# A diffusion backbone on one core: products and row sums of the adaLN chunks tied to TensorE's progress

## The chip, the cores and the metric

The kernel runs on one core of one Trainium2 chip. The metric is the device time of one execution in microseconds (us). A core has TensorE (PE, matmuls into PSUM), VectorE (DVE), ScalarE (ACT), GpSimd (POOL) and SyncE (SP), which here issues all transfers between HBM and SBUF. Each engine works through its own instructions in order, and semaphores tie the engines together.

## The reference

Two layers over 512 latent tokens of width 1024: layer 0 mixes with windowed attention (256 context tokens beside it), layer 1 with a short gated convolution. Each layer is

```
sh1, sc1, g1, sh2, sc2, g2 = split(silu(c) @ ada_w[i] + ada_b[i])      # six chunks of 1024
h = h + g1 * mixer(rms_norm(h) * gain * (1 + sc1) + sh1)
a = rms_norm(h) * gain * (1 + sc2) + sh2
g, u = split(dwconv3(a @ w_up))                                         # 2 x 2816 wide
h = h + g2 * ((silu(g) * u) @ w_down)
```

All is in float32. The six chunks of a layer (the adaLN modulation) are the product of one vector, silu(c), with a 1024 x 6144 matrix. This text is about seven of these chunks, the last of layer 0 (g2) and all six of layer 1.

## The kernel before

Activations are kept transposed, with features on the 128 partitions and the 512 tokens along the free dimension; h is 8 tiles of 128x512. Each float32 operand of a large matmul is split into a high and a low part (`split`, L163: ScalarE casts to `hi`, VectorE subtracts to get `lo`), and one block product is three matmuls (`mm3`, L195 to L198). A weight tile of 128x1024 is loaded by SP into `wraw` (4 buffers, L172) and split into `whi` and `wlo` (4 + 3 buffers during the FFNs, `wpiece`, L177).

Up to L670 the start and the window attention run in an order written out by hand. Behind that, from the output projection to the end, the order on each engine is made by the framework's scheduler, which follows the program's order as a priority and places an instruction earlier where its engine is free and its inputs are ready by its own reckoning. An instruction with a dependency on another can't be placed ahead of it, and waits for it on a semaphore.

The stretch around the change, in order:

- The output projection of the attention (`out_proj` called at L799). Its first four tiles come from weights at hand; then `last_cols` (L787) closes a chunk of layer 0. It ends by spreading silu(c) over all partitions as a row, `crow` (128x1024): eight TensorE transposes into two PSUM banks and two ScalarE copies (L792 to L796). The last four tiles run in two halves of 256 tokens, and in the second half the norm of the first half begins (`norm_half`, L741; `rstd`, L209, with a root on ScalarE; `modulate`, L230, with VectorE at L233 and L235 and ScalarE at L234). The sums of squares of the first tiles are added on POOL (L207), those of the others on VectorE.
- The first FFN (`ffn`, L801). The 22 pairs of hidden tiles (j and j + 22) are done in thirds of 8, 8 and 6 pairs. A pair is two up projections of 24 matmuls (the first two pairs together, in halves, with the norm's second half hooked in), a convolution over tokens of each (`conv`, L724: ScalarE L725, VectorE L726 and L727), a silu (L818), a product (L819) and a split (L821). After each third the down projection (`out_proj` at L828) runs over its hidden tiles into 8 output tiles, each added into h on VectorE (L736). PSUM has 8 banks, taken in turn (`nbank`).
- The chunks beside it. `adaq` (L677) lists 7 x 8 tiles, each 128 columns of a chunk. For a tile, `ada_tile` (L679) loads 512 KB of transposed weights into one of three buffers `araw` and multiplies them by `crow` on POOL (L684); `ada_sum` (L691) sums the rows on ScalarE, with an activation that has an accumulator (L694), and behind a chunk's eighth tile VectorE adds the bias (L696). `tail0` (L833) is called with 2 after each pair but the first and with 1 after each down tile of the first two thirds. For each tile it first writes out the sums of all products but the last one, then the next product. Only the very first product has a dependency, on the last `modulate` of the norm so far.
- `after_ffn0` (L841) writes out the sums that are left and makes layer 1's scales; the rest of layer 1 (gated convolution, second FFN) uses the same loops without chunk work.

Of the kernel before, what the change touches and what calls it, by code (L numbers as in the profile page):

```python
# [9 lines left out]
DEP = mybir.DependencyInfo(mybir.DependencyClass.Sync, mybir.DependencyReason.DATA)  # L10
AF = mybir.ActivationFunctionType
# [3 lines left out]
P = 128  # L15
# [3 lines left out]
KT = D // P  # L19
# [75 lines left out]
def kernel(ctx: ExitStack, tc: tile.TileContext, xT, ctxT, par_d, rope_d, mask_d, ident_d,  # L95
                         ada0_d, ada_d, adat_d, wqkv_d, wo_d, wup_d, wdown_d, wsc_d, wsco_d, out_d):
    nc = tc.nc
    vec, act, pool, pe, sp = nc.vector, nc.scalar, nc.gpsimd, nc.tensor, nc.sync
# [8 lines left out]
    def nm(s):  # L107
        uid[0] += 1
        return f"{s}{uid[0]}"
# [4 lines left out]
    def bank(tag):  # L114
        if tag == "s":
            return spool[0].tile([P, 512], F32, tag="s", name=nm("ps_s"), bufs=4)
        return pp.tile([P, 512], F32, tag=tag, name=nm("ps_" + tag), bufs=BANKS[tag])
# [7 lines left out]
    def nbank():  # L125
        t = ring[ringpos[0] % 8]
        ringpos[0] += 1
        return bank(t)
# [12 lines left out]
    ident = cp.tile([P, P], F32, name="ident")  # L141
# [7 lines left out]
    cs = cp.tile([P, KT, 2], F32, name="cs")  # L149

    def pc(name, i, n=1):
        o = PC[name][0] + i
        return par[:, o:o + n]
# [41 lines left out]
    def mm3(ps, wh, wl, ah, al, start, stop):  # L195
        pe.matmul(out=ps, lhsT=wh, rhs=ah, start=start, stop=False)  # L196
        pe.matmul(out=ps, lhsT=wh, rhs=al, start=False, stop=False)  # L197
        pe.matmul(out=ps, lhsT=wl, rhs=ah, start=False, stop=stop)  # L198

    def sumsq_add(acc, x, first, eng):  # L200
        if first:
# [41 lines left out]
    def ada_transpose(acc, ps):  # L243
        for i in range(4):
            pe.transpose(out=ps[:, i * P:(i + 1) * P], in_=acc[:, i * P:(i + 1) * P], identity=ident)
        return ps

    def ada_columns(ch, half, ps):
        col = ada[0][:, ch, half * 4:half * 4 + 4]
        vec.tensor_reduce(out=col, in_=ps.rearrange("p (a b) -> p a b", a=4), axis=AX.X, op=ALU.add)  # L250
        vec.tensor_tensor(out=col, in0=col, in1=pc("adab", ch * KT + half * 4, 4), op=ALU.add)

    def scale_cols(dst, sc, gain):
        vec.scalar_tensor_tensor(out=dst, in0=sc, scalar=1.0, in1=gain, op0=ALU.add, op1=ALU.mult)
# [417 lines left out]
    with tc.tile_pool(name="ffn", bufs=1, reuse_waits="tile") as fp, four_banks() as sp3:  # L672
# [3 lines left out]

        adaq = [(0, 5, m) for m in range(KT)] + [(1, ch, m) for ch in (1, 0, 4, 3, 2, 5) for m in range(KT)]  # L677

        def ada_tile(after=None):  # L679

            layer, ch, m = adaq.pop(0)
            w = fp.tile([P, 1024], F32, tag="araw", name=nm("araw"), bufs=3)
            sp.dma_start(out=w, in_=adat_d[6 * layer + ch - 5, m])
            ins = pool.tensor_tensor(out=w, in0=w, in1=crow, op=ALU.mult)  # L684
            if after is not None:
                tc.add_manual_dep(ins.ins, after.ins.name, DEP, reason="the norm has VectorE's port for itself")
            adaps.append((layer, ch, m, w))

        adaps = []

        def ada_sum():  # L691
            layer, ch, m, w = adaps.pop(0)
            col = ada[layer][:, ch, :]
            act.activation(out=w, in_=w, func=AF.Copy, accum_out=col[:, m:m + 1])  # L694
            if m == KT - 1:
                vec.tensor_tensor(out=col, in0=col, in1=pc("adab", (layer * 6 + ch) * KT, KT), op=ALU.add)  # L696

# [9 lines left out]
        def proj(pieces, ah, al, halves=False, group=None, hook=None):  # L707

            n = len(pieces)
            nk = len(ah)  # L710
            group = n if group is None else group
            banks = [nbank() for _ in pieces]
            for hf in (HALVES if halves else (FULL,)):
                for m0 in range(0, n, group):
                    for kt in range(nk):
                        if hook is not None and kt == HOOK_AT and hf.start == 0:
                            hook()
                        ks = slice(kt * P, (kt + 1) * P)
                        for m in range(m0, m0 + group):
                            wh, wl = pieces[m]  # L720
                            mm3(banks[m][:, hf], wh[:, ks], wl[:, ks], ah[kt][:, hf], al[kt][:, hf], kt == 0, kt == nk - 1)
            return banks
# [15 lines left out]
        def norm_begin(slot, shift):  # L738
            return {"acc": f(), "slot": slot, "shift": shift, "ah": [at() for _ in range(KT)], "al": [at() for _ in range(KT)]}
# [6 lines left out]
        def out_proj(src, n, ah, al, gate, nxt=None, last=False, lead=(), tail_w=None, after=None, cols=None):  # L746
# [26 lines left out]
            for hf in HALVES:  # L773
                for i, m in enumerate(ms):
                    if nxt is not None and hf.start and i == HALF_AT:
                        norm_half(nxt, HALVES[0])
                    for kt in range(nk):
                        ks = slice(kt * P, (kt + 1) * P)
                        mm3(banks[i][:, hf], pieces[i][0][:, ks], pieces[i][1][:, ks], ah[kt][:, hf], al[kt][:, hf], kt == 0, kt == nk - 1)
                    residual(m, banks[i], gate, hf)  # L780
                    done(m, hf)
# [3 lines left out]
        crow = fp.tile([P, 1024], F32, name="crow")  # L785

        def last_cols():  # L787
            banks = [ada_transpose(accs[2, hf], nbank()) for hf in range(2)]
            for hf in range(2):
                ada_columns(4, hf, banks[hf])  # L790
            scale_cols(smod[:, 2, :], ada[0][:, 4, :], pc("gffn", 0, 8))
            for half in range(2):  # L792
                ps = nbank()
                for i in range(4):
                    pe.transpose(out=ps[:, i * P:(i + 1) * P], in_=cs[:, half * 4 + i, 0:1].broadcast_to([P, P]), identity=ident)
                act.copy(out=crow[:, half * 512:(half + 1) * 512], in_=ps)  # L796

        nf = norm_begin(2, ada[0][:, 3, :])
        out_proj(lambda m: wo_d[m], 1024, o_hi, o_lo, ada[0][:, 2, :], nf, False, lead, lead_tail, cols=last_cols)  # L799

        def ffn(layer, ah, al, tail, nxt, second):  # L801
# [26 lines left out]
                out_proj(lambda m: wdown_d[layer, m, :, j0 * P:j1 * P], (j1 - j0) * P, hh, hl, gate, nx, fin, after=None if fin else tail)  # L828
            return nx

        held = [True]

        def tail0(n):  # L833
            for _ in range(n):
                while len(adaps) > 1 or adaps and not adaq:
                    ada_sum()
                if adaq:
                    ada_tile(nf["end"] if held else None)
                    held.clear()

        def after_ffn0():  # L841
            assert not adaq
            while adaps:
                ada_sum()
            scale_cols(smod[:, 3, :], ada[1][:, 1, :], pc("gmix", 8, 8))
            scale_cols(smod[:, 4, :], ada[1][:, 4, :], pc("gffn", 8, 8))
            return norm_begin(3, ada[1][:, 0, :])

        n1 = ffn(0, nf["ah"], nf["al"], tail0, after_ffn0, lambda: norm_half(nf, HALVES[1]))
        ah, al = n1["ah"], n1["al"]  # L850

# [91 lines left out]
```

## Time and profile before

| | |
|---|---|
| time, median of 3 runs | 1251.68 us (1250.4 to 1255.4) |
| profiled execution, its own time | 1252.96 us |
| its span, first to last instruction | 1251.2 us |
| mean granted TensorE clock | 0.984 |
| busy: PE, DVE, ACT, POOL | 1196.5, 744.7, 540.3, 302.1 us |
| products of the chunks (L684, POOL) | 56, 150.0 us |
| row sums of the chunks (L694, ACT) | 56, 59.2 us |

The profile is one execution taken by the hardware profiler. A busy time counts an engine's instructions, with waits for a port inside an instruction included; idle time is put down to the instruction that released the engine. In rows of the timeline the columns are start, duration, engine, line, operation, output <- inputs, and in brackets the idle time ahead of it and its releaser. In rows of groups they are line, engine, operation, names, shapes and count, then busy time and mean duration in ns, then the idle time ahead and what ended it. Rows of waits have the total, the count and the longest. PEld is the loading of weights, which overlaps the matmuls. Some matmul records are missing from a trace, so counts of matmuls in a window are good to a few per cent.

### The profile page before, as it was taken

To read this page: it belongs to the slowest core of one execution; us is meant where nothing else is said; L and a number is where in the kernel's file an instruction comes from. 1 tells how busy PE (TensorE), PEld (TensorE's weight loads), DVE (VectorE), ACT (ScalarE), POOL (GpSimd) and SP (SyncE) were. 2 spreads that over 40 slices of the span, in tenths; PEclk is the share of its full clock that TensorE was granted. 3 is DMA by queue.
4 is the path that set the end of the run, shared out by engine and by line. 5 is a ranking of instruction groups with operands and counts; after the bars stand their busy time and mean duration, and the time that the engine had idled before them with its cause. 6 is when DMAs were issued, how large, how long until landed. Compare 5 with 4: busy or idle time off the path is not lost.

```text
span 1251.2 us, 16317 instructions
## 1 busy us (share of the span) xinstructions
PE 1196.5 (96%) x6366; PEld 978.2 (78%) x6366; DVE 744.7 (60%) x1107; ACT 540.3 (43%) x899; POOL 302.1 (24%) x204
## 2 busy tenths in 40 slices
PE   8999999996997499999999999999999999999998
PEld 6676666696886288888888988889988888888888
DVE  4688788658677745663455754444686446553552
ACT  4434777536656554432334442232454224422430
POOL 0069598425638893000001000001000000000000
PEclk9999999998999599999999999999999999999999
DMA  9445143345467674332323233322243333332211
GB/s 361 158 153 171 60 152 118 97 161 171 145 235 229 227 265 144 111 101 86 92 76 105 81 118 101 93 92 69 67 143 93 101 95 91 102 101 85 79 39 68
DMA packets 50317, 157.60 MB, mean 126 GB/s; under 512 B 5696, under 2 KB 7744, under 8 KB 50240
## 3 DMA queue, kind: packets, MB, share of 16 engines
q1 hardware_dynamic: 50240, 156.56, 38.9%
q8 instruction: 50, 0.82, 0.3%
q14 instruction: 27, 0.22, 0.1%
HBM read 152.86 MB, written 2.10 MB: 124 GB/s over the span
## 4 chain that ended last, share of the span: by engine, by line
PE 78%; DVE 7%; issue 4%; POOL 4%; ACT 3%; DMA 3%; SPq 0%; POOLq 0%; DVEq 0%; ACTq 0%
PE ps_s L197 11%; PE ps_s L198 11%; PE ps_s L196 11%; PE ps_pt L196 5%; PE ps_pt L198 5%; PE ps_pt L197 5%; PE ps_oa L629 3%; PE ps_pt L610 3%; PE ps_oa L196 3%; PE ps_oa L197 3%; PE ps_oa L198 3%; PE ps_qt L198 3%; PE ps_qt L197 3%; PE ps_qt L196 3%; DMA araw<-in_adat 3%
## 5 line engine op out<-in xcount | busy, mean ns | idle before, releaser
L165 DVE TENSOR_TENSOR wlo<-wraw,whi 128x1024 fp32r<-128x1024 f32 (+2 forms) x194 | 226.4, 1175 | 186.9 <-ACT whi L164 182.4
L164 ACT CAST whi<-wraw 128x1024 fp32r<-128x1024 f32 (+2 forms) x194 | 183.1, 952 | 284.5 <-PE ps_s L197 124.2
L197 PE MATMUL ps_s<-a,whi 128*128 128x512 f32 (+1 forms) x480 | 176.7, 368 | 0.0
L198 PE MATMUL ps_s<-a,wlo 128*128 128x512 f32 (+1 forms) x480 | 176.5, 368 | 0.0
L196 PE MATMUL ps_s<-a,whi 128*128 128x512 f32 (+1 forms) x480 | 176.5, 368 | 0.0
L684 POOL TENSOR_TENSOR araw<-araw,crow 128x1024 f32<-128x1024 f32 x56 | 150.0, 2700 | 62.6 <-DMA araw<-in_adat 59.7
L196 PE MATMUL ps_s<-g,whi 128*128 128x512 f32 (+1 forms) x296 | 107.1, 362 | 22.2 <-ACT g L164 22.2
L197 PE MATMUL ps_s<-g,whi 128*128 128x512 f32 (+1 forms) x296 | 106.6, 361 | 3.7 <-DVE g L165 3.7
L198 PE MATMUL ps_s<-g,wlo 128*128 128x512 f32 (+1 forms) x296 | 106.1, 359 | 0.0
L198 PEld LDWEIGHTS ps_s<-a,wlo 128*128 128x128 f32 x480 | 90.5, 188 | 15.1
L197 PEld LDWEIGHTS ps_s<-a,whi 128*128 128x128 f32 x480 | 90.5, 188 | 14.9
L196 PEld LDWEIGHTS ps_s<-a,whi 128*128 128x128 f32 x480 | 90.4, 188 | 14.9
L197 PE MATMUL ps_pt<-a,whi 128*128 128x512 f32 (+1 forms) x256 | 94.8, 370 | 2.5 <-DVE a L235 2.5
L207 POOL TENSOR_TENSOR f<-f,t 128x512 f32<-128x512 f32 x6 | 9.5, 1580 | 359.1 <-ACT t L206 359.1
L196 PE MATMUL ps_pt<-a,whi 128*128 128x512 f32 (+1 forms) x256 | 94.7, 370 | 0.7 <-ACT a L234 0.7
L198 PE MATMUL ps_pt<-a,wlo 128*128 128x512 f32 (+1 forms) x256 | 94.5, 369 | 0.0
L694 ACT ACTIVATE araw<-araw 128x1024 f32<-128x1024 f32 x56 | 59.2, 1057 | 60.7 <-POOL araw L684 60.4
L196 PEld LDWEIGHTS ps_s<-g,whi 128*128 128x128 f32 x296 | 57.5, 194 | 32.0 <-ACT g L164 23.4
L736 DVE SCALAR_TENSOR_TENSOR h<-ps_s,ada,h 128x512 f32<-128x512 f32 (+1 forms) x44 | 28.5, 651 | 88.7 <-PE ps_s L198 88.7
L164 ACT CAST g<-f 128x512 fp32r<-128x512 f32 x52 | 32.2, 620 | 99.5 <-DVE f L819 98.9
L197 PEld LDWEIGHTS ps_s<-g,whi 128*128 128x128 f32 x296 | 57.4, 194 | 13.6 <-DVE g L165 4.9
L198 PEld LDWEIGHTS ps_s<-g,wlo 128*128 128x128 f32 x296 | 57.4, 194 | 8.3
(301 smaller groups left out, 2592.8 us busy)
## 6 DMA issues: line engine op xcount, KB each, us to landing
wraw<-in_wup SPq DMA_DIRECT2D x88, 512.0 KB, 3.6
araw<-in_adat SPq DMA_DIRECT2D x56, 512.0 KB, 4.0
wraw<-in_wdown SPq DMA_DIRECT2D x32, 512.0 KB, 3.6
araw<-in_ada SPq DMA_DIRECT2D x48, 256.0 KB, 2.7
wraw<-in_wsc SPq DMA_DIRECT2D x24, 512.0 KB, 3.6
gw<-in_ada SPq DMA_DIRECT2D x16, 512.0 KB, 10.2
wraw<-in_wqkv SPq DMA_DIRECT2D x12, 512.0 KB, 7.0
wraw<-in_wdown SPq DMA_DIRECT2D x16, 384.0 KB, 3.1
```

Source lines behind the costliest of these rows:

```text
L164: act.copy(out=hi, in_=raw)
L165: vec.tensor_tensor(out=lo, in0=raw, in1=hi.bitcast(F32), op=ALU.subtract)
L196: pe.matmul(out=ps, lhsT=wh, rhs=ah, start=start, stop=False)
L197: pe.matmul(out=ps, lhsT=wh, rhs=al, start=False, stop=False)
L198: pe.matmul(out=ps, lhsT=wl, rhs=ah, start=False, stop=stop)
L207: eng.tensor_tensor(out=acc, in0=acc, in1=sq[:, :n], op=ALU.add)
L610: pe.transpose(out=pt[:, q:q + P], in_=es[p, b, t][0][:, o:o + P], identity=ident)
L629: pe.matmul(out=r["po"][HALF[t], b0:b0 + n], lhsT=V[:, j, p // 2, :], rhs=pf[:, t * n:(t + 1) * n], start=first, stop=not r["left"])
L684: ins = pool.tensor_tensor(out=w, in0=w, in1=crow, op=ALU.mult)
L694: act.activation(out=w, in_=w, func=AF.Copy, accum_out=col[:, m:m + 1])
L736: vec.scalar_tensor_tensor(out=h[m][:, cl], in0=ps[:, cl], scalar=gate[:, m:m + 1], in1=h[m][:, cl], op0=ALU.mult, op1=ALU.add)
```

## The change

Each product and each row sum gets a dependency on a matmul. `mm3` keeps its last matmul in `lastmm`; `tail0` passes the one written last, which is the last of the up tile or down tile behind which it is called. At each call the sums of all products so far come first and then the new products, so that a sum is one call behind its product. The spread of silu(c) leaves `last_cols` and is written out at the first call of `tail0`, behind the first two pairs. The old dependency of the first product on the norm goes.

```diff
-        pe.matmul(out=ps, lhsT=wl, rhs=ah, start=False, stop=stop)
+        lastmm[0] = pe.matmul(out=ps, lhsT=wl, rhs=ah, start=False, stop=stop)
...
-        def ada_tile(after=None):
+        def ada_tile(after):
...
             ins = pool.tensor_tensor(out=w, in0=w, in1=crow, op=ALU.mult)
-            if after is not None:
-                tc.add_manual_dep(ins.ins, after.ins.name, DEP, reason="the norm has VectorE's port for itself")
+            pace(ins, after)
             adaps.append((layer, ch, m, w))
...
+        def pace(ins, after):
+            tc.add_manual_dep(ins.ins, after.ins.name, DEP, reason="not ahead of TensorE")
+
-        def ada_sum():
+        def ada_sum(after):
...
-            act.activation(out=w, in_=w, func=AF.Copy, accum_out=col[:, m:m + 1])
+            pace(act.activation(out=w, in_=w, func=AF.Copy, accum_out=col[:, m:m + 1]), after)
...
             scale_cols(smod[:, 2, :], ada[0][:, 4, :], pc("gffn", 0, 8))
-            for half in range(2):
-                ps = nbank()
-                for i in range(4):
-                    pe.transpose(...)
-                act.copy(out=crow[:, half * 512:(half + 1) * 512], in_=ps)
...
-        held = [True]
+        def spread_c():
+
+            for half in range(2):
+                ps = nbank()
+                for i in range(4):
+                    pe.transpose(out=ps[:, i * P:(i + 1) * P], in_=cs[:, half * 4 + i, 0:1].broadcast_to([P, P]), identity=ident)
+                act.copy(out=crow[:, half * 512:(half + 1) * 512], in_=ps)
 
         def tail0(n):
+
+            if len(adaq) == 7 * KT:
+                spread_c()
+            while adaps:
+                ada_sum(lastmm[0])
             for _ in range(n):
-                while len(adaps) > 1 or adaps and not adaq:
-                    ada_sum()
                 if adaq:
-                    ada_tile(nf["end"] if held else None)
-                    held.clear()
+                    ada_tile(lastmm[0])
 
         def after_ffn0():
             assert not adaq
             while adaps:
-                ada_sum()
+                ada_sum(lastmm[0])
```

The code of `spread_c` is that which stood in `last_cols`.

More of the change, by code (lines that the diff above doesn't have):

```diff
@@ L197, in mm3 @@
         pe.matmul(out=ps, lhsT=wh, rhs=al, start=False, stop=False)
-        pe.matmul(out=ps, lhsT=wl, rhs=ah, start=False, stop=stop)
+        lastmm[0] = pe.matmul(out=ps, lhsT=wl, rhs=ah, start=False, stop=stop)
+    lastmm = [None]
     def sumsq_add(acc, x, first, eng):
@@ L791, in last_cols @@
             scale_cols(smod[:, 2, :], ada[0][:, 4, :], pc("gffn", 0, 8))
-            for half in range(2):
-                ps = nbank()
-                for i in range(4):
-                    pe.transpose(out=ps[:, i * P:(i + 1) * P], in_=cs[:, half * 4 + i, 0:1].broadcast_to([P, P]), identity=ident)
-                act.copy(out=crow[:, half * 512:(half + 1) * 512], in_=ps)
         nf = norm_begin(2, ada[0][:, 3, :])
```

## The prediction

> **What bounds the kernel now.** I read the page's busy row and forty slices first, then windows cut at the stages of the first FFN, then the waits engine by engine, and last the timelines around the holes. The slices of PE and of its clock:
>
> ```profile
> PE   8999999996997499999999999999999999999998
> PEclk9999999998999599999999999999999999999999
> ```
>
> TensorE is full almost everywhere, so only a hole in its row can be won. There are two after the start: slices 9 to 11 and slices 12 and 13, the second with the granted clock down. The windows (us, busy time of PE, PEld, DVE, ACT, POOL with instruction counts, clock, DMA share, GB/s) put numbers on them:
>
> ```profile
> 280.00:330.00 50.00, 37.82 (x287) 36.33 (x286) 37.89 (x54) 28.12 (x57) 29.11 (x12) 0.93 0.53 175
> 330.00:395.00 65.00, 65.00 (x288) 53.83 (x287) 47.05 (x53) 41.72 (x67) 40.03 (x16) 1.00 0.63 205
> 395.00:434.00 39.00, 13.08 (x37) 8.73 (x36) 31.32 (x22) 23.26 (x38) 32.55 (x12) 0.61 0.65 224
> 434.00:484.00 50.00, 50.00 (x218) 40.54 (x217) 18.01 (x18) 27.80 (x43) 43.08 (x17) 1.00 0.73 242
> 484.00:660.00 176.00, 176.00 (x773) 144.68 (x772) 99.13 (x119) 63.09 (x83) 0.00 (x0) 1.00 0.32 93
> ```
>
> 280 to 330 is the norm ahead of the first FFN: 50 - 37.8 = 12.2 us idle, and a clock of 0.93, which is 0.07 x 37.8 = 2.6 us at most; I count 2. At 395 to 434 the first third of the hidden tiles is done and the down projection starts. The row above it gives the pace, 65 / 288 = 0.226 us a matmul; 37 matmuls need 8.4 us, so 39 - 8.4 = 30.6 us are lost, idleness and half clock together; I count 30. **Together 44 us**, the most that packing this stretch can give. Who made TensorE wait, from 255 to 650 us:
>
> ```profile
> PE ps_s L196 <- ACT g L164: 22.2, 2, 14.9
> PE ps_pt L225 <- DVE rcol L222: 5.2, 1, 5.2
> PE ps_s L197 <- DVE g L165: 3.7, 2, 3.2
> PE ps_s L215 <- DVE f L207: 2.9, 1, 2.9
> ```
>
> The 22.2 and 3.7 are the hidden tiles of the last pairs (L819 to L821), late at ScalarE and VectorE. Their lateness comes from the chunk work in between:
>
> ```profile
> ACT araw L694 <- POOL araw L684: 60.4, 38, 4.2
> POOL araw L684 <- DMA araw<-in_adat: 59.7, 23, 10.6
> L684 POOL TENSOR_TENSOR araw<-araw,crow x56: 2340/2490/4386, 268.7 to 478.6; 128x1024 f32<-128x1024 f32 x56
> L694 ACT ACTIVATE araw<-araw x56: 1041/1061/1066, 271.6 to 481.2; 128x1024 f32<-128x1024 f32 x56
> ```
>
> All 56 products run between 268.7 and 478.6, though the code puts their last behind the fifth pair of the last third. They are pulled ahead of TensorE, and ScalarE, which works in order, waits 60 us for products that wait 60 us for transfers. What that does to the hidden tiles stands in ScalarE's timeline:
>
> ```profile
> 409.06 1.06 ACT L694 ACTIVATE araw<-araw 128x1024 f32<-128x1024 f32 x1 [2.53 <-POOL araw L684]
> 412.33 1.06 ACT L694 ACTIVATE araw<-araw 128x1024 f32<-128x1024 f32 x1 [2.13 <-POOL araw L684]
> 413.39 0.60 ACT L164 CAST g<-f 128x512 fp32r<-128x512 f32 x1
> 414.05 0.80 PE L196 MATMUL ps_s<-g,whi 128*128 128x512 f32 x1 [14.88 <-ACT g L164]
> ```
>
> The cast for which TensorE stood 14.88 us ran right behind two sums that waited for POOL. The control is the rest of the kernel: from 640 to 1251 us, with two norms and the whole second FFN of the same loops, and no chunk work, TensorE waited three times in all:
>
> ```profile
> PE ps_s L225 <- POOL rcol L219: 0.9, 2, 0.5
> PE ps_pt L225 <- POOL rcol L219: 0.5, 1, 0.5
> PE ps_qt L225 <- POOL rcol L219: 0.4, 1, 0.4
> ```
>
> **The change part by part.** Durations are from one execution of 1252.96 us (span 1251.2 and 1.8 around it), 0.1% above the median 1251.68.
>
> *Products and sums wait for a matmul.* No instruction is added, only waits; 29 calls of the tail function carry them: 2 chunk tiles behind a pair of up tiles (7, 8 and 5 calls), 1 behind a down tile (8 and 8): 14 + 8 + 16 + 8 + 10 = 56. A product can no longer start before the pair that it stands behind, so the norm runs without POOL, and the work ends about 54 tiles x 24 x 0.226 = 293 us after the first call, near 615 us.
>
> The norm. VectorE's slow operations go, and ScalarE's way to the root is shorter:
>
> ```profile
> 296.44 2.62 DVE L235 SCALAR_TENSOR_TENSOR a<-t,ada,a 128x256 fp32r<-128x256 f32 x1
> 299.76 0.47 DVE L235 SCALAR_TENSOR_TENSOR a<-t,ada,a 128x256 fp32r<-128x256 f32 x1
> 287.25 1.06 ACT L694 ACTIVATE araw<-araw 128x1024 f32<-128x1024 f32 x1 [3.29 <-POOL araw L684]
> 290.81 1.28 ACT L221 ACT_TABLE_LOAD   x1
> ```
>
> The 2.62 us one overlaps a product, the 0.47 one doesn't. Without the 3.29 us wait and the two sums ahead of the table load, about 5.7 us, the 5.2 us stall falls to nothing or to one of the control's 0.5; the table load stays on the path, so I leave 1 us there and 2 for the rest: **3 of 14 us remain**.
>
> The end of the first third. ScalarE's cast of the last hidden tile now finds ahead of it only the sums of the products one call earlier. Behind a waiting sum on ScalarE stand the conversions of later weights and the next convolution; the convolution waits for the same matmul, and the weights sit seven deep. Behind a waiting product on POOL stands nothing until the next norm. The sums of two tiles, 2 x 1.06 and two reads of the accumulator, run while VectorE has its share of the convolution and the product, 2 x 0.75 + 0.69 = 2.2 us by the rows below; I leave **1 us** for what sticks out here, and charge 1 us to the end of the second third, which had none before and now has products beside it. The third third issues no product behind its last pair.
>
> *Room for the chunk work beside TensorE.* VectorE by line and shape, with POOL quiet (first four rows, 490 to 560), with POOL busy in the hole (fifth, 400 to 430) and with POOL at 43 of 50 us in the down tiles (sixth, 434 to 480):
>
> ```profile
> L165 DVE TENSOR_TENSOR wlo<-wraw,whi 128x1024 fp32r<-128x1024 f32 x14 | 17.2, 1225 | 18.6 <-ACT whi L164 18.6
> L727 DVE SCALAR_TENSOR_TENSOR f<-ps_s,par,f 128x511 f32<-128x511 f32 x7 | 5.2, 750 | 0.2
> L819 DVE TENSOR_TENSOR f<-f,f 128x512 f32<-128x512 f32 x7 | 4.8, 693 | 0.2
> L165 DVE TENSOR_TENSOR g<-f,g 128x512 fp32r<-128x512 f32 x7 | 4.8, 692 | 4.8 <-ACT g L164 4.8
> L165 DVE TENSOR_TENSOR wlo<-wraw,whi 128x1024 fp32r<-128x1024 f32 x4 | 10.8, 2698 | 0.9 <-ACT whi L164 0.9
> L165 DVE TENSOR_TENSOR wlo<-wraw,whi 128x1024 fp32r<-128x1024 f32 x7 | 10.0, 1425 | 17.8 <-ACT whi L164 17.7
> L727 DVE SCALAR_TENSOR_TENSOR f<-ps_pt,par,f 128x511 f32<-128x511 f32 x2 | 1.5, 750 | 0.1
> ```
>
> The last row is again from 400 to 430. A pair costs TensorE 48 x 0.226 = 10.8 us. VectorE needs 2 x 1.23 + 4 x 0.75 + 0.69 + 0.69 = 6.8 us for it, POOL 2 x 2.49 = 5.0. What slows beside POOL is the kind without PSUM (1225 to 2698 ns); L727, which reads PSUM, takes 750 either way. So per pair 3.8 + 5.0 = 8.8 us can't overlap, under 10.8: cost 0. If nothing of VectorE's overlapped, 6.8 + 5.0 = 11.8 would be 1.0 us over, 20 us in 20 calls: the upper end. Below nothing there is no end, since those tiles run gapless now. I take 0, by the down-tile window, where TensorE was busy 50.00 of 50 beside denser POOL work.
> By the Trainium skill ("SBUF — State Buffer", section "Who interferes with whom"), a VectorE instruction with two SBUF inputs and a GpSimd one that reads SBUF shut each other out for a whole instruction, and one with a single SBUF input doesn't contend. The rows bear it out; it speaks against spreading, since each product may now hold up a split beside a busy VectorE, and for the sum it gives the 8.8 us case, not the 11.8.
>
> *The transfers.* SP issues each chunk tile when its buffer is free, that is after the sum of three tiles before; the weights' transfers stand behind it. Demand is 4 x 512 KB in 10.8 us, 194 GB/s; the window at 434 moved 242. For the second tile of a call the path is the sum with its read of the accumulator, the transfer with its median of 4.0, and the product, 2.5:
>
> ```profile
> L694 ACT ACTIVATION_READ_ACCUMULATOR araw<-araw x56: 181/185/190, 272.5 to 482.2; 128x1 f32 x56
> araw<-in_adat SPq DMA_DIRECT2D x56, 512.0 KB, 4.0
> ```
>
> 1.06 + 0.18 = 1.2, and 1.2 + 4.0 + 2.5 = 7.7 us, 3 us within the pair. Cost 0; without that cover see the slower rival.
>
> *The row of c.* Eight transposes and two copies move behind the first four up tiles:
>
> ```profile
> 265.62 0.60 PE L795 MATMUL ps_pt<-ident,cs 128*128 128x128 f32 x4
> 266.05 0.60 PE L795 MATMUL ps_qt<-ident,cs 128*128 128x128 f32 x4
> 334.46 0.67 ACT L725 ACTIVATE f<-ps_pt,par 128x512 f32<-128x512 f32 x1
> ```
>
> 1.2 us of TensorE on either side cancels. But they take two banks, so the next up tile gets the first bank of that group, busy until its convolution is read: 0.67 on ScalarE and 2 x 0.75 on VectorE, 2.2 us, of which the group's other matmuls and the transposes hide 1 to 2. Bounds 0 and 2.2; I take 1.5, as both engines come out of the norm with work left.
>
> **Sum.** Won 44; left over 3 + 1 + 1 + 1.5 = 6.5. Net 37: 1252.96 - 37 = **1216 us**. Bounds: nothing left over, 1209, or 1208 from the median; everything left over plus half of the 20 us, 1226.
>
> **Rivals.** *VectorE and POOL exclude each other wholly, or part of the stalls stays*: 1216 + 20 = 1236 (1226 to 1245). For it: 2698 ns in the hole. Against: L727, and the 50.00 of 50.
> *The paced work stops running ahead, but the holes had another cause*, late weights or the norm's own length: time as now, 1246 to 1258. Against: the three short waits of the control and the sums ahead of the cast at 413.39.
> *Slower: ScalarE waits at each sum for a late product.* With three buffers the second tile's transfer starts only after a sum that itself waits for TensorE; if that chain of 7.7 us slips past 10.8, every call stalls the convolutions. The 60.4 / 38 = 1.6 us mean wait over 20 calls is 32 us, 1248; the 4.2 us longest is 84, 1300. It decides for slower from (37 + 6) / 20 = 2.2 us a call; at 2.9, halfway, 1274. For it: the chain's 3 us of slack is thin. Against: a wait must exceed what the banks and the seven weights ahead absorb.
>
> **How the numbers follow.** Forecast (1208 to 1226) 0.68; exclusion or partial 0.17; as now 0.07; slower 0.08. The range 1208 to 1236 takes in the forecast and most of the second case, and leaves out 0.2. A measurement tells 0.5%, 6 us, from no change: faster 0.84, same 0.08, slower 0.08.
>
> **What would show it.** Right: L684 from about 320 to 615; no wait of TensorE over 2 us from 280 to 434; clock 1.00 there; ScalarE's wait for POOL far under 60 us. Wrong: L819 and the splits at over 2 us in the up tiles with holes in TensorE (first rival); the hole at the third's end with no sum ahead of the cast (second); ScalarE idle for POOL at each call, and TensorE behind it (third).

## The result and the profile after

The changed kernel takes 1213.34 us (median, 1212.34 to 1215.51) against 1252.34 beside it: a ratio of 0.9689, 95% interval 0.9665 to 0.9713, or 39 us less. The forecast was 1216, with 1208 to 1236 as its range. The span of the profiled execution fell from 1251.2 to 1211.3 us.

The page of the changed kernel, busy tenths of TensorE and its clock in 40 slices:

```profile
PE   8999999999999999999999999999999999999998
PEclk9999999999999999999999999999999999999999
```

Both holes are closed. The same windows as before, in the same columns (us, busy PE, PEld, DVE, ACT, POOL with counts, clock, DMA share, GB/s):

```profile
280.00:330.00 50.00, 48.57 (x348) 45.69 (x347) 39.02 (x73) 31.32 (x59) 9.01 (x3) 1.00 0.23 74
330.00:395.00 65.00, 63.86 (x280) 52.19 (x280) 49.95 (x49) 37.37 (x59) 32.86 (x14) 1.00 0.62 215
395.00:434.00 39.00, 39.00 (x170) 31.54 (x169) 23.10 (x16) 15.39 (x22) 17.77 (x7) 1.00 0.66 209
434.00:484.00 50.00, 50.00 (x223) 41.40 (x222) 36.23 (x37) 27.79 (x44) 22.41 (x9) 1.00 0.51 169
484.00:660.00 176.00, 173.52 (x811) 144.16 (x810) 119.22 (x124) 86.51 (x137) 66.84 (x29) 0.99 0.51 165
```

At 280 to 330 TensorE is idle for 1.4 us instead of 12.2, at 395 to 434 for none. POOL's work is now spread: 9 us in the norm's window instead of 29, and 67 us in the last window, where it had none. The waits, TensorE's from 255 us to the end (first two of five rows) and ScalarE's for POOL, and the products of the chunks by line (min, median and max in ns, first and last start):

```profile
PE ps_s L196 <- ACT g L164: 3.1, 2, 2.0
PE ps_oa L196 <- ACT crow L836: 1.4, 1, 1.4
```

```profile
ACT araw L698 <- POOL araw L686: 3.0, 3, 1.2
```

```profile
L686 POOL TENSOR_TENSOR araw<-araw,crow x56: 2378/2412/5092, 315.5 to 625.2; 128x1024 f32<-128x1024 f32 x56
```

ScalarE waits 3.0 us for products instead of 60.4, and the products run to 625 us instead of 479. What is left of TensorE's waiting in the first FFN is 1.4 us at the first full up tile, 1.1 us at the end of the first third and 2.0 us at the end of the second. The other three rows, 1.8 us in all, are the short waits of the later norms that the kernel before has too.

### The profile page after: what moved, and what is told of

Its sections match the earlier page's. It is cut to its first block, busy times and chain, and to the rows that moved or that the text cites. A ratio compares the mean times of both kernels' runs of the same rounds, so it can differ in the third digit from the quotient of the medians.

```text
span 1211.3 us, 16338 instructions
## 1 busy us (share of the span) xinstructions
PE 1190.3 (98%) x6366; PEld 974.5 (80%) x6366; DVE 752.4 (62%) x1107; ACT 536.6 (44%) x899; POOL 296.4 (24%) x204
## 4 chain that ended last, share of the span: by engine, by line
PE 84%; DVE 8%; ACT 3%; issue 2%; POOL 2%; DMA 0%; SPq 0%; POOLq 0%; ACTq 0%; DVEq 0%
PE ps_s L196 11%; PE ps_s L198 11%; PE ps_s L197 11%; PE ps_pt L197 6%; PE ps_pt L198 6%; PE ps_pt L196 6%; DVE wlo L165 3%; PE ps_oa L631 3%; PE ps_pt L612 3%; PE ps_oa L196 3%; PE ps_oa L197 3%; PE ps_oa L198 3%; PE ps_qt L197 3%; PE ps_qt L198 3%; PE ps_qt L196 3%
## 5 line engine op out<-in xcount | busy, mean ns | idle before, releaser
L165 DVE TENSOR_TENSOR wlo<-wraw,whi 128x1024 fp32r<-128x1024 f32 (+2 forms) x194 | 264.3, 1371 | 165.8 <-ACT whi L164 160.5
L197 PE MATMUL ps_s<-a,whi 128*128 128x512 f32 (+1 forms) x448 | 167.6, 374 | 0.0
L196 PE MATMUL ps_s<-a,whi 128*128 128x512 f32 (+1 forms) x448 | 167.6, 374 | 0.0
L198 PE MATMUL ps_s<-a,wlo 128*128 128x512 f32 (+1 forms) x448 | 167.5, 374 | 0.0
L196 PE MATMUL ps_s<-g,whi 128*128 128x512 f32 (+1 forms) x264 | 95.9, 364 | 3.1 <-ACT g L164 3.1
L196 PEld LDWEIGHTS ps_s<-a,whi 128*128 128x128 f32 x448 | 84.4, 188 | 15.0
L197 PEld LDWEIGHTS ps_s<-a,whi 128*128 128x128 f32 x448 | 84.4, 188 | 14.9
L198 PE MATMUL ps_s<-g,wlo 128*128 128x512 f32 (+1 forms) x264 | 96.0, 364 | 0.0
L197 PE MATMUL ps_s<-g,whi 128*128 128x512 f32 (+1 forms) x264 | 95.8, 364 | 0.0
L817 ACT ACTIVATE f<-f 128x512 f32<-128x512 f32 x44 | 27.9, 633 | 81.9 <-DVE f L731 81.8
L560 DVE CUSTOM_DVE_ANT_0 e<-ps_s,mask,nsink 128x640 f32<-128x640 f32 (+1 forms) x64 | 53.7, 874 | 11.1 <-PE ps_s L551 10.7
L698 ACT ACTIVATE araw<-araw 128x1024 f32<-128x1024 f32 x56 | 58.7, 1052 | 3.0 <-POOL araw L686 3.0
L196 PEld LDWEIGHTS ps_s<-g,whi 128*128 128x128 f32 x264 | 49.9, 189 | 12.4 <-ACT g L164 4.0
L196 PEld LDWEIGHTS ps_pt<-a,whi 128*128 128x128 f32 x272 | 51.3, 189 | 8.1
```

The source lines that it names most:

```text
L165: vec.tensor_tensor(out=lo, in0=raw, in1=hi.bitcast(F32), op=ALU.subtract)
L198: lastmm[0] = pe.matmul(out=ps, lhsT=wl, rhs=ah, start=False, stop=stop)
L560: vec.tensor_tensor_reduce(out=e[:, :n].rearrange("p (a b) -> p a b", a=np_), in0=s[:, :np_, :w], in1=mb.rearrange("p (a b) -> p a b", a=n ...
L698: pace(act.activation(out=w, in_=w, func=AF.Copy, accum_out=col[:, m:m + 1]), after)
L817: act.activation(out=cv[0], in_=cv[0], func=AF.Silu)
```

## The experiments

Ratios are to the kernel before, run on the same chip.

**Two losses, or one? (r4)** The kernel before, with every product held to the end of the norm:

```diff
-                    ada_tile(nf["end"] if held else None)
-                    held.clear()
+                    ada_tile(nf["end"])
```

> The kernel before, but every product, not the first alone, waits for the last modulate of the norm; nothing is tied to a matmul. Theory (two separate losses, 14 us in the norm and 30 us at the end of the first third): the norm's loss falls to 0 to 3 us, the hole at the end of the first third stays with 20 us or more: 1234 to 1246. Rival (one loss only, the head start in the norm caused the backlog behind it): both go, 1213 to 1222. Second rival: the work held back in the norm lands on the first third and the hole grows by as much: 1248 to 1255.

1243.65 us, ratio 0.9929 (0.9906 to 0.9952). TensorE's waits from 255 to 700 us in this kernel, the two longest rows:

```profile
PE ps_s L196 <- ACT g L164: 27.2, 3, 11.9
PE ps_s L197 <- DVE g L165: 1.9, 2, 1.7
```

The norm's waits of 5.2 and 2.9 us are gone (TensorE is busy 50.00 of 50 us at 280 to 330), and the waits for hidden tiles have grown, from 22.2 + 3.7 to 27.2 + 1.9 us. So there were two losses. With the norm's alone taken away, 9 of the 39 us are won, after a part of it has come back as waits for hidden tiles.

**Order or dependency? (r3)** As changed, with neither product nor sum tied to a matmul:

```diff
-            pace(ins, after)
...
-            pace(act.activation(out=w, in_=w, func=AF.Copy, accum_out=col[:, m:m + 1]), after)
+            act.activation(out=w, in_=w, func=AF.Copy, accum_out=col[:, m:m + 1])
```

> Neither products nor sums wait for a matmul; the sums still come one call behind their products in the program, and the spread stays behind the first pairs. Theory (the dependencies are what holds the work back, the order in the program isn't): products run ahead again once the row of c is there, the hole at the end of the first third is back with 15 to 30 us, while the norm stays free of products: 1228 to 1243, products finished long before 625 us. Rival (writing the sums one call later is what helps): 1213 to 1217.

1258.57 us, ratio 1.0044 (1.0025 to 1.0063): the hole is back, but the time is outside what was expected, 0.4% above that of the kernel before. By line, and TensorE's longest wait:

```profile
L686 POOL TENSOR_TENSOR araw<-araw,crow x56: 2338/2650/3392, 317.8 to 511.5; 128x1024 f32<-128x1024 f32 x56
```

```profile
PE ps_s L196 <- ACT g L164: 41.7, 5, 12.6
```

All 56 products are pressed into 194 us behind the norm instead of 210 us that began in it. What the norm gained was paid back in the first two thirds: 41.7 us of waits for hidden tiles instead of 22.2. That is the mechanism of the second rival written for r4; there it took back only a part, here all of it.

**Which of the two dependencies? (r1, r2)** r1 leaves out the second `pace` above (sums free), r2 the first (products free).

> Only the products wait for a matmul, the sums don't; order and spread as changed. Theory (the run-ahead of the products made the holes; a sum can't be ahead of its product): 1213 to 1218, ratio to before about 0.97, no wait of TensorE over 3 us. Rival (the sums' own wait keeps them from standing in ScalarE's queue ahead of the convolution while POOL is still at work): ScalarE again waits for POOL for tens of us, holes at the ends of the thirds of 5 us and more, 1220 to 1235.

1228.80 us, ratio 0.9819 (0.9804 to 0.9833): the rival held. ScalarE's waits for POOL, then TensorE's longest:

```profile
ACT araw L698 <- POOL araw L686: 45.1, 30, 2.2
```

```profile
PE ps_s L196 <- ACT g L164: 13.1, 3, 7.1
```

> Only the sums wait for a matmul, the products don't; order and spread as changed. Theory: with three buffers a product can be at most three tiles ahead of the sums, so pacing the sums paces the products too, and no sum finds its product unfinished: 1212 to 1216. Rival (each needs its own wait): 1220 or more.

1213.46 us, ratio 0.9697 (0.968 to 0.9714): the time of the whole change, and ScalarE's wait for POOL is 2.6 us. Tying the sums alone is enough: with three buffers the products stay near them, and run to 626.9 us in r2 against 625.2 in the changed kernel. Tying the products alone leaves 15 us on the table: a free sum is placed on ScalarE right behind its product and waits for it, 1.5 us in the mean, with the next convolution behind.

**Any matmul, or a later one? (r10, r5)** In r10 each sum is written in its own product's call and waits for that call's matmul:

```diff
-            while adaps:
-                ada_sum(lastmm[0])
             for _ in range(n):
                 if adaq:
                     ada_tile(lastmm[0])
+            while adaps:
+                ada_sum(lastmm[0])
```

> As changed, but each sum is written in the call of its own product, behind it, and waits for that call's matmul. Theory (what helps is that a sum waits for the matmul of a later tile than its product's, which leaves the transfer and the product a call's time): as the products alone in r1, 1225 to 1232, ScalarE waits for POOL some 45 us in all, the hole at the first third's end 5 us and more. Rival (any wait on a matmul does it): 1213 to 1217.

1228.73 us, ratio 0.9812 (0.9796 to 0.9828), and ScalarE's wait for POOL is 45.1 us in 30 waits, as in r1. A sum's wait helps only if it is on the matmul of a later call: that gives transfer and product the time of a call. r5 was meant to show the same with the sums written by the old rule:

```diff
-            while adaps:
-                ada_sum(lastmm[0])
             for _ in range(n):
+                while len(adaps) > 1 or adaps and not adaq:
+                    ada_sum(lastmm[0])
```

> Products and sums wait as changed, but the sums are written as before, all but the newest product's ahead of each new product, so that the first sum of a call belongs to a product of the same call. Theory: ScalarE then waits in every up call for a transfer and a product behind the same matmul, some 6 us in 10.8, with the next convolution behind it; the last hidden tile of the first two thirds comes 4 to 8 us later and ScalarE runs short: 1220 to 1245, its wait for POOL 60 us or more. Rival (ScalarE has room enough, 5.5 of 10 us busy): 1213 to 1217.

1213.66 us, ratio 0.9699 (0.9683 to 0.9715): no change, and the expectation was wrong about the code. The old rule holds back the newest product's sum, so after two products both are still open, and both sums come in the next call, tied to its matmul. The old order already had its sums one call late; what it lacked was the wait that made it so on the chip.

**The ends of the thirds (r7).** No chunk tile is issued behind the last two pairs of the first and of the second third; the first four down tiles of each take two instead:

```diff
-                        tail(2)
+                        tail(0 if j in (6, 7, 14, 15) else 2)
...
-                    after(1)
+                    after(2 if m < 4 else 1)
```

> No chunk tile is issued behind the last two pairs of the first and second third; the eight tiles go behind the first four down tiles of each (two instead of one). Theory: the 1.1 and 2.0 us at the ends of the thirds are splits of weights that VectorE runs at 2.6 us beside a product instead of 1.23, ahead of the last convolution in its queue; both waits go, the split there takes 1.23 us, and the time is about 3 us shorter, 1210. Rival: the waits come from the sums on ScalarE, or the denser down tiles give them back: 1213 to 1216.

The reason for it is the timeline of the changed kernel at the end of the first third (start, duration, engine, line):

```profile
378.29 4.80 POOL L686 TENSOR_TENSOR araw<-araw,crow 128x1024 f32<-128x1024 f32 x2 [6.02 <-DMA araw<-in_adat]
381.54 2.63 DVE L165 TENSOR_TENSOR wlo<-wraw,whi 128x1024 fp32r<-128x1024 f32 x1 [1.70 <-ACT whi L164]
384.10 0.73 DVE L730 SCALAR_TENSOR_TENSOR f<-ps_qt,par,f 128x511 f32<-128x511 f32 x1
387.05 0.50 PE L196 MATMUL ps_s<-g,whi 128*128 128x512 f32 x1 [1.14 <-ACT g L164]
```

The split of a weight tile, 1.23 us when POOL is quiet, takes 2.63 beside the products, and the last convolution stands behind it on VectorE. ScalarE's part of that convolution (L729) was done ahead of the two sums (L698):

```profile
381.41 0.68 ACT L729 ACTIVATE f<-ps_qt,par 128x512 f32<-128x512 f32 x1
381.99 1.05 ACT L698 ACTIVATE araw<-araw 128x1024 f32<-128x1024 f32 x1
```

The split and the convolution behind it in r7:

```profile
381.21 1.23 DVE L165 TENSOR_TENSOR wlo<-wraw,whi 128x1024 fp32r<-128x1024 f32 x1 [2.77 <-ACT whi L164]
382.35 0.75 DVE L730 SCALAR_TENSOR_TENSOR f<-ps_qt,par,f 128x511 f32<-128x511 f32 x1
```

r7 takes 1208.80 us, ratio 0.9648 (0.9633 to 0.9662), beside r0's 1213.17. TensorE no longer waits for a hidden tile. It is 4.4 us faster than the change and, with r9, the fastest kernel here. Behind the last pair there are neither products nor sums in r7; that the split decides, and not the sums, is read from the timelines and not from a run of its own.

**The place of the spread (r6, r9).** r6 moves the eight transposes and two copies of `spread_c` back to the end of `last_cols`; r9 does that and what r7 does.

> The spread of silu(c) goes back into last_cols, all else as changed. Theory: the 1.43 us that TensorE waits at the first full up tile is a PSUM bank whose convolution isn't read yet, and comes from the two banks that the spread takes behind the first pairs; it goes, and the time is 1.4 us shorter, ratio to the changed kernel 0.9988 (1212). Rival: the wait is the end of the convolution whatever the bank, and stays: 1213.3.

1215.34 us, ratio 0.9698 (0.9684 to 0.9711) beside r0's 0.9686 (0.967 to 0.9702): nothing won. The 1.4 us wait at the first full up tile is gone, as expected, but those for hidden tiles grew from 3.0 to 5.2 us:

```profile
PE ps_s L196 <- ACT g L164: 5.2, 2, 3.0
```

> r6 and r7 together: the spread back in last_cols, and no chunk tile behind the last two pairs of the first and second third. Theory: in r6 the 1.4 us won at the first full up tile only moved to the end of the first third, where the last convolution was late by VectorE's queue and not by TensorE; with that end free of products the 1.4 us is kept: no wait of TensorE over 0.6 us in the first FFN, 1207.4 against r7's 1208.8 (ratio to before 0.9637). Rival (the spread behind the first pairs costs nothing in time): as r7, or 1 to 2 us slower.

1208.62 us, ratio 0.9651 (0.9637 to 0.9666): TensorE's waits in the first FFN are gone except for one of 0.3 us and the two of the norm behind it, as expected, but the time can't be told from r7's. That fits convolutions which set the end of the third in r6, so that TensorE, earlier there, only waits longer; that r9 keeps the 1.4 us isn't shown by its time. Whether that wait is for the bank's convolution or for the copy of `crow`, which the profile names, stays open, since no run parted them. By the code the tile needs its bank and not `crow`, and in the changed kernel VectorE's last reading of that bank (L731 on `ps_oa`) ends at 314.87 us, 0.14 us ahead of the tile's first matmul; but a copy of `crow` ends at nearly the same time.

**How much room is left for POOL (r8).** Ahead of each chunk tile two more products of half the size, into a scratch tile that nothing reads:

```diff
+            for _ in range(2 * n if adaq else 0):
+                pace(pool.tensor_tensor(out=pscr, in0=crow[:, 0:512], in1=crow[:, 512:1024], op=ALU.mult), lastmm[0])
```

> POOL's work beside the first FFN is doubled: ahead of each chunk tile two extra products of 128x512 into a scratch tile that nobody reads, tied to the same matmul. Theory of the forecast (two-input operations of VectorE without PSUM and POOL shut each other out, 3.8 + 5.0 = 8.8 us of a pair's 10.8): now 3.8 + 9.9 = 13.7 us, over by 2.9 us a pair, so VectorE's splits rise well over 2 us, and the time rises by something up to 20 x 2.9 = 58 us: 1225 to 1270. If VectorE only waits for the half-size product in progress (1.2 us a piece), at the low end. Rival (they mostly overlap): 1213 to 1217, with holes no bigger than now.

1255.15 us, ratio 1.0025 (1.0014 to 1.0037): 42 us more than r0, and more than the 39 that the change had won. Two windows of r8, the second half of the first third's up tiles and the start of its down projection:

```profile
330.00:384.00 54.00, 54.00 (x240) 44.70 (x239) 46.45 (x40) 26.27 (x41) 47.91 (x24) 1.00 0.55 187
384.00:410.00 26.00, 11.36 (x35) 7.90 (x34) 18.40 (x16) 13.34 (x21) 25.61 (x13) 0.67 0.48 161
```

TensorE is full to the end of the third and then stands, as in the kernel before. VectorE's product of the convolutions, from 460 to 515 us, in r0 and in r8, and in r8 the operation that reads PSUM (count, then busy us and mean ns):

```profile
L818 DVE TENSOR_TENSOR f<-f,f 128x512 f32<-128x512 f32 x5 | 3.5, 693 | 0.1
```

```profile
L819 DVE TENSOR_TENSOR f<-f,f 128x512 f32<-128x512 f32 x5 | 11.0, 2197 | 0.1
L731 DVE SCALAR_TENSOR_TENSOR f<-ps_s,par,f 128x511 f32<-128x511 f32 x5 | 3.8, 750 | 0.2
```

The product with both inputs in SBUF went from 693 to 2197 ns, the operation that reads PSUM takes 750 either way. The Trainium skill ("SBUF — State Buffer", section "Who interferes with whom") says that a VectorE instruction with two SBUF inputs contends with a GpSimd one that reads SBUF, and these rows agree. At twice the POOL work the pair no longer fits its 10.8 us: if all 42 us are put down to the 20 up calls, it is over by 42 / 20 = 2.1 us on average, against the 2.9 reckoned. Late products add to it (ScalarE waits 50.9 us for POOL in r8); the run doesn't part the two.

**The changed kernel again (r0),** as the base for r6 to r8:

> The changed kernel again, beside the next two on the same chip: 1213 us (1211 to 1216) by every theory. Three waits of TensorE for the first FFN's side work, as in its first profile: 1.4 us at the first full up tile, 1.1 and 2.0 us where the first and the second third end.

1213.17 us, ratio 0.9686 (0.967 to 0.9702), TensorE's waits 3.0 and 1.4 us.

## Why the prediction was right

*44 us to win.* Right: in r4 and r3 the norm's part goes while the other stays, and the windows after show both closed.

*3 us left in the norm.* Too much: TensorE has no wait there at all. With POOL quiet, ScalarE comes to the root at once, and its table load lies between the two small steps of TensorE (L217 and L227), which matmuls fill:

```profile
282.35 0.50 PE L217 MATMUL ps_s<-ones,f 128*128 128x1 f32 x4
285.17 0.38 PE L227 MATMUL ps_s<-ident,rcol 128*128 128x128 f32 x2
```

```profile
283.07 1.28 ACT L223 ACT_TABLE_LOAD   x1
```

*1.5 us at the first full up tile.* 1.4 measured. r6 shows that the moved spread causes it, and that putting the spread back won no time by itself.

*1 us at the end of each of two thirds.* 1.1 and 2.0 us, and around the second a lower clock, by the window of the changed kernel:

```profile
520.00:530.00 10.00, 8.82 (x31) 6.99 (x32) 5.71 (x6) 5.24 (x8) 6.72 (x3) 0.83 0.71 249
```

That is another 8.8 x 0.17 = 1.5 us in this execution; in r0's profile the second wait is 1.8 us and the clock there stays at 1.00. So 2 us were forecast and 4.6 came, and the reason was another: the forecast put it on the sums on ScalarE, and the timelines put it on a split that VectorE runs beside a product.

The leftovers measured are 1.4 + 1.1 + 2.0 + 1.5 = 6.0 instead of 6.5, so the sum lands at 44 - 6 = 38, against 39 by the medians. That the total came so near is in part luck: 3 us too much in the norm and 2.6 too little at the ends of the thirds nearly cancel.

*Cost 0 for the chunk work beside TensorE.* Right for the up loops: no hole inside a third. The 8.8 us reckoned for two-input operations and products in a pair of 10.8 left 2 us of room, and r8 shows that doubled POOL work no longer fits. The exclusion rival is borne out for VectorE's operations with two inputs in SBUF. It is not for those that read PSUM, 750 ns in r8 too, so its 11.8 us, in which nothing overlaps, counted too much.

*The slower rival* didn't come about: ScalarE waits three times, 3.0 us in all. A ScalarE that waits at the sums is seen in r1 and r10, for another reason than the rival's chain through the buffers: there a sum doesn't wait for a later call's matmul and comes right behind its product. The waits are 1.5 us in the mean, near the rival's 1.6, but they cost 15 us and not its 32, less than the change wins.

*Where the reading was incomplete:* the forecast named the products' run-ahead as the cause and gave the two dependencies no separate price. r2 shows that the sums' dependency alone is enough for all of it, r1 that the products' alone is worth 23 of the 39 us, and r5 that the rewritten order carries nothing.

*The cast at 413.39* was read as held up by two sums. That is the smaller part of it there: its input, the product of L819, ended only at 412.85, behind a slow split, by VectorE's timeline of the kernel before:

```profile
407.08 3.02 DVE L165 TENSOR_TENSOR wlo<-wraw,whi 128x1024 fp32r<-128x1024 f32 x1
410.03 2.82 DVE L819 TENSOR_TENSOR f<-f,f 128x512 f32<-128x512 f32 x1
```

At the 1.23 and 0.69 us that they take with POOL quiet, the two would have been 3.9 us shorter; the sum held the cast for another 0.5. Ahead of them a convolution on ScalarE (L725) had come late behind sums. So both ScalarE's waits and VectorE's slow operations made the hole. r1 puts 15 us on ScalarE's waits with the products paced; no run has the slow operations alone with products as dense as there.

*Two counts* are wrong in the forecast, and nothing rests on them: the tail function is called with chunk tiles 20 + 16 = 36 times, not 29, and the three rows of the control are four waits.

## What to carry to other kernels

By r10 against the changed kernel, side work on an in-order engine should wait for a point of the main work that is later than the point where its own input starts; a wait on the same point leaves the engine standing until that input is there. By r2 a bounded set of buffers then paces the producers by itself. By r8 a full bottleneck engine doesn't show that its helpers keep up: the debt comes due where the stage's last result is needed, so leave side work out of the last steps ahead of such a point.

## What was not expected

TensorE can hide a lag of the convolutions for half a third: in r8 it runs 54.00 of 54 us while VectorE falls behind, and pays with 26 - 35 x 0.226 = 18 us, idleness and lower clock together, at 384 to 410. Moving work out of one stage without holding it back (r3) cost as much in the next as it won, and a little more.
